# Hybrid decoder block: every engine and the load queue held to the order in which the kernel is written

## The chip, the cores and the metric

The kernel runs on one core of one Trainium2 chip. The metric is device time in microseconds (us) of one execution; several executions are timed and their median is given. One execution was profiled besides, and its trace is what the rows below come from. A core has TensorE (PE, with its weight loads PEld), VectorE (DVE), ScalarE (ACT), GpSimd (POOL) and SyncE (SP), which here issues nearly all DMAs and is called the load queue.

## The reference

One decoder block on 512 tokens of width 2048, behind 16 meta tokens, in fp32. Two branches share one input projection; their outputs are merged by sigmoid gates and projected.

```python
u = rmsnorm(h, norm_g)                      # h = [meta | x], 528 tokens
q, k, v, g_att, z_ssm, xbc, dt, m_att, m_ssm = split(u @ w_in)
# differential attention, 8 heads, ALiBi, causal; p = softmax of each of two maps
oa = rmsnorm(einsum(p[0] - lam * p[1], v), subln_g) * (1 - lam_init)
y_att = (oa * silu(g_att)) @ w_br_attn
# SSD (Mamba-2), 32 heads, chunks of 128 tokens
xbc = silu(causal_conv4(xbc) + conv_b)
xs, bm, cm = split(xbc)
dtf = softplus(dt + dt_bias)
ys = ssd_chunked(xs, dtf, -exp(a_log), bm, cm) + xs * d_skip
y_ssm = rmsnorm_groups(ys * silu(z_ssm), ssm_norm_g) @ w_br_ssm
h = h + (sigmoid(m_att) * y_att + sigmoid(m_ssm) * y_ssm) @ w_out
out = rmsnorm(h[16:], final_g)
```

## The kernel before

**Dense work.** All weights lie in one array of tiles of 128x1024, loaded by the load queue into five buffers `w` (`pump`, `release`). A product in fp32 is three matmuls: each operand is split into a high part and a remainder, and high*high, high*low and low*high are summed in PSUM. `split` (L173, L174) makes `wh` on ScalarE and `wl` on VectorE for half a tile, five buffers each; `xsplit` (L438, L439) does the same for the token operands `xv`. A job of most matrices is one level of Strassen (`strassen`): seven products P1 to P7 over quarter operands B11, B12, B21, B22 and their differences T1 to T4, with weight sums S on VectorE (L184, L187). A unit is half a product, 12 matmuls (L310); a `plain` job has units of 24 (L354).

**Order of the work.** `dense` runs a job's units through a look-ahead: two units have their weight sums written ahead (SUMS), three their weight split (LOOK), then the unit's matmuls are written. `later(fn, n)` writes a function n units on; side work (attention heads, the SSD chunks) is a list of generators, `tasks`, and one or more steps of them are written behind each unit. `flush` empties the look-ahead, `drain` the side tasks; a stage ends with them, and a stage's set-up code follows. The context is built with `TileContext(schedule_with_timeline_sim=True)`: what is written is a sequence for each engine, but a scheduler chooses in which order each engine issues its instructions.

**Stages** in the profile's time: token norms and q/k/v/gate jobs with eight attention heads beside them (up to some 600 us), the convolution jobs (to some 860), z jobs with the SSD chunks beside (to some 1340), the last gate jobs, the jobs ya (attention branch) and ys (SSM branch, to some 1620), the out jobs, and the final norm.

**Places that the change and the prediction touch.**
- `token_scale(n)`: squares of the tokens on ScalarE (L508), power -0.5 on POOL, a broadcast by TensorE (L527), a copy to `y` on ScalarE (L529); then VectorE scales the quarters `q_B..` (L541) and `xsplit` splits them.
- `attn_out`: squares of the head's output (L783), sums (L786 to L788), power on POOL (L789), scaling to `og` (L792), transposes by TensorE (L796), gating (L798). `head_tasks` puts a head's steps into `tasks`; `run_unit` posts it six units after the head's last dense unit. `qk_parts` splits q and k.
- the set-up of the SSD stage (L897 to L961): constants, `dt` loaded back (L913), transposes (L922, L924), softplus as a series on VectorE (L925 to L946), cumulative sums by TensorE (L948, L949), exponentials, transposes (L958), a copy and a store (L960, L961). It is written between the convolution's `flush` and the first z job.
- `ssd_group`/`chunk`: a chunk's decay matrices `mm` on ScalarE (L1049, eight, with six more ScalarE operations in the same step).
- `ssm_operands`: side task beside the ya jobs that loads and splits the ys jobs' operands. `out_operand`: splits the out jobs' operands from the merged tiles `mq` (m11, m12, m21, m22); the first six of eight rows of each quarter are split during the last ys job, the rest behind it.

```python
def out_operand(v, *parts):
...
        for o in parts:
            if p is not None:
                (psub if v in ("T2", "T3") else vsub)(d[:, o], p[:, o], m[:, o])
            xsplit(xo[v], d[:, o], o, pool if v == "B22" and o.start == 0 and p is None else dve)
```

## Time and profile before

| | before |
|---|---|
| time, median of 3 runs | 1818.43 us (1816.68 to 1822.35) |
| profiled execution: time, span | 1816.67 us, 1815.0 us |
| mean granted clock of TensorE | 0.973 of full speed |
| instructions | 35924 |
| TensorE / VectorE / ScalarE / POOL busy | 94% / 86% / 53% / 14% of the span |
| chain that ended last | TensorE 68%, VectorE 18%, DMA 5% |

The span is from the first to the last instruction of the profiled execution. Busy time of TensorE is modelled from its records, so busy does not mean full rate: a lower granted clock shows as the same busy time with fewer matmuls. Names in rows are the program's tiles, output before the arrow; L310 is line 310 of the kernel before.

### The profile page before, as it was taken

What the parts mean: (1) busy time and instruction counts of PE and PEld (TensorE: products, weight loads), DVE (VectorE), ACT (ScalarE), POOL (GpSimd) and SP (SyncE); (2) the same over time, 40 slices, a digit from 0 to 9 for tenths busy, and PEclk for the clock granted to TensorE, in tenths of its full rate; (3) what the DMA queues carried; (4) which work ended last, traced back from release to release, by engine and by line L of the source; (5) the groups of instructions that cost most, each with busy time, mean ns of one, the idle gap of its engine ahead of it and who ended that gap; (6) DMA issues with size and microseconds to landing.
All of it is one profiled execution on the core that took longest, in us unless ns stands there. A gap on an engine that the chain in (4) does not pass through costs nothing.

```text
span 1815.0 us, 35924 instructions
## 1 busy us (share of the span) xinstructions
PE 1707.7 (94%) x13547; PEld 1639.2 (90%) x13547; DVE 1565.0 (86%) x3004; ACT 969.2 (53%) x1961; POOL 262.1 (14%) x241
## 2 busy tenths in 40 slices
PE   5999999999999799999998999999998999989995
PEld 4999988988989799999997889989998999989995
DVE  6898878887888699999988888988978499999996
ACT  6555545554565355555576665555553254455553
POOL 0000000000000000000013431121302012235443
PEclk9999989998999899999999999999999999999998
DMA  7332212221223134333556555455466545433433
GB/s 298 134 113 82 88 64 88 70 89 65 88 76 106 66 129 129 129 118 129 154 172 177 172 156 171 158 169 167 127 231 228 186 144 171 153 114 106 139 117 105
DMA packets 136765, 244.10 MB, mean 134 GB/s; under 512 B 15088, under 2 KB 78768, under 8 KB 136080
## 3 DMA queue, kind: packets, MB, share of 16 engines
q1 hardware_dynamic: 136592, 241.81, 40.9%
q8 instruction: 107, 1.75, 0.4%
q14 instruction: 66, 0.54, 0.1%
HBM read 207.88 MB, written 33.88 MB: 133 GB/s over the span
## 4 chain that ended last, share of the span: by engine, by line
PE 68%; DVE 18%; DMA 5%; issue 4%; ACT 4%; POOL 1%; SPq 0%; DVEq 0%; ACTq 0%; POOLq 0%
PE d_ps L310 53%; PE d_ps L354 6%; DVE wl L174 5%; DMA w<-in_w_all 2%; DVE w L184 2%; DVE cv L865 2%; DMA mm<-d_acs 2%; PE s_ps L722 1%; ACT wh L173 1%; DVE S L187 1%; PE o_ps L770 1%; ACT mm L1049 1%; DVE u L187 1%; PE s_ps L719 1%; DVE S L184 1%
## 5 line engine op out<-in xcount | busy, mean ns | idle before, releaser
L310 PE MATMUL d_ps<-x,wh 128*128 128x256 f32 (+1 forms) x4160 | 772.2, 286 | 16.2 <-ACT x L438 5.9
L310 PEld LDWEIGHTS d_ps<-x,wh 128*128 128x128 f32 x4160 | 647.9, 191 | 24.7 <-ACT x L438 6.3
L173 ACT ACTIVATE wh<-w 128x512 fp32r<-128x512 f32 x706 | 438.3, 628 | 407.1 <-PE d_ps L310 263.0
L310 PE MATMUL d_ps<-x,wl 128*128 128x256 f32 (+1 forms) x2080 | 593.1, 287 | 11.1 <-DVE wl L174 10.7
L174 DVE TENSOR_TENSOR wl<-w,wh 128x512 fp32r<-128x512 f32 x706 | 506.5, 729 | 109.7 <-ACT wh L173 105.5
L310 PE MATMUL d_ps<-y,wh 128*128 128x256 f32 (+1 forms) x3120 | 585.8, 287 | 8.4 <-ACT wh L173 5.2
L310 PEld LDWEIGHTS d_ps<-y,wh 128*128 128x128 f32 x3120 | 488.3, 191 | 18.9 <-ACT wh L173 8.0
L310 PE MATMUL d_ps<-y,wl 128*128 128x256 f32 (+1 forms) x1560 | 444.4, 287 | 0.6 <-DVE wl L174 0.5
L310 PEld LDWEIGHTS d_ps<-x,wl 128*128 128x128 f32 x2080 | 393.7, 190 | 17.9 <-DVE wl L174 15.0
L310 PEld LDWEIGHTS d_ps<-y,wl 128*128 128x128 f32 x1560 | 296.1, 191 | 3.9 <-DVE wl L174 1.7
L173 ACT ACTIVATE wh<-S 128x512 fp32r<-128x512 f32 x260 | 158.7, 627 | 154.6 <-PE d_ps L310 73.5
L174 DVE TENSOR_TENSOR wl<-S,wh 128x512 fp32r<-128x512 f32 x260 | 182.3, 716 | 23.6 <-ACT wh L173 21.5
L354 PE MATMUL d_ps<-x,wh 128*128 128x256 f32 x704 | 129.3, 284 | 2.1 <-DVE cth L1170 1.1
L354 PEld LDWEIGHTS d_ps<-x,wh 128*128 128x128 f32 x704 | 109.5, 191 | 3.3 <-ACT y L438 1.3
L354 PE MATMUL d_ps<-x,wl 128*128 128x256 f32 x352 | 99.2, 286 | 5.5 <-DVE wl L174 5.4
L184 DVE TENSOR_TENSOR S<-S,w 128x512 f32<-128x512 f32 x130 | 94.6, 766 | 0.0
L184 DVE TENSOR_TENSOR w<-w 128x512 f32<-128x512 f32 x130 | 92.3, 719 | 0.0
L184 DVE TENSOR_TENSOR w<-w,S 128x512 f32<-128x512 f32 x130 | 88.3, 693 | 1.1
L187 DVE TENSOR_TENSOR S<-w 128x512 f32<-128x512 f32 x130 | 86.8, 707 | 2.4 <-DMA w<-in_w_all 2.0
L789 POOL TENSOR_TENSOR ssq<-ssq,mhalf 128x4 f32<-128x4 f32 x8 | 8.1, 1007 | 514.2 <-DVE ssq L788 514.2
L354 PEld LDWEIGHTS d_ps<-x,wl 128*128 128x128 f32 x352 | 66.4, 190 | 6.6 <-DVE wl L174 6.2
L190 POOL TENSOR_TENSOR mq<-mq,cth 128x256 f32<-128x256 f32 x32 | 36.5, 1152 | 194.5 <-DVE mq L187 191.0
(258 smaller groups left out, 1849.2 us busy)
## 6 DMA issues: line engine op xcount, KB each, us to landing
w<-in_w_all SPq DMA_DIRECT2D x291, 512.0 KB, 3.6
mm<-d_acs SPq DMA_DIRECT2D x16, 512.0 KB, 6.5
d_x<-cv SPq DMA_DIRECT2D x24, 264.0 KB, 2.0
q_B<-in_xT SPq DMA_DIRECT2D x8, 528.0 KB, 11.8
d_tha<-gth SPq DMA_DIRECT2D x16, 256.0 KB, 3.1
lx<-d_x SPq DMA_DIRECT2D x16, 256.0 KB, 4.5
d_sz<-gth SPq DMA_DIRECT2D x16, 256.0 KB, 4.3
lz<-d_sz SPq DMA_DIRECT2D x16, 256.0 KB, 3.5
```

The lines of the kernel that those rows point to most:

```text
L173: act.activation(h[:, :n], src, AF.Copy)
L174: dve.tensor_tensor(l[:, :n], src, h[:, :n].bitcast(F32), ALU.subtract)
L184: dve.tensor_tensor(dst, a, b, ALU.subtract)
L187: dve.tensor_tensor(dst, a, b, ALU.add)
L190: pool.tensor_tensor(dst, a, b, ALU.mult)
L310: pe.matmul(ps[:, :width], lhsT=a[:, ks], rhs=x[:, kk, lo:lo + width], start=(kk == 0 and i == 0), stop=(kk == kp - 1 and i == 2))
L354: pe.matmul(b[:, :width], lhsT=a[:, cs], rhs=x[:, ki, lo:lo + width], start=(first and k == 0 and i == 0), stop=(last and k == 1 and i == 2))
L719: pe.matmul(ps[:, :b - a], lhsT=qs[:, m, rows], rhs=ks[:, m, a:b], start=True, stop=False)
L722: pe.matmul(ps[:, :b - a], lhsT=qs[ms, m, rows], rhs=kl[ms, a:b], start=False, stop=True)
L770: pe.matmul(o_ps[:, i, :], lhsT=at[:, j, :], rhs=vt[:, j, :], start=(j == 0), stop=False)
L865: dve.scalar_tensor_tensor(v, raw[:, j:j + L], cw[:, ft, j:j + 1], v, ALU.mult, ALU.add)
L1049: act.activation(mm[:, h, :], mm[:, h, :], AF.Relu, scale=-1.0, bias=acs[:, c, g * HPG + h:g * HPG + h + 1])
```

## The change

`InOrder` wraps the five issuing engines: each instruction gets a dependency on the one written before it on the same engine, of a class that needs no semaphore (NoSync). The scheduler may therefore no longer move an instruction past another on its engine or on the load queue. Besides, some code is written at other places: head tasks are posted four units after a head's last dense unit and not six; `qk_parts` makes k's parts first; the z job's tanh is posted two units later for one of its four quarters; the last gate job uses its seven products in another order (ORDER_LAST); the subtractions T2 and T3 of the ys and out operands, and one remainder of B22, go from POOL to VectorE; other slots hold B21 and T3 of out; B21 and B22 of the ys operands are no longer split beside the ya jobs but at units 1 to 4 of the first ys job (`soon`, `ssm_late`).

```diff
+ORDER_LAST = ("P1", "P2", "P6", "P7", "P4", "P3", "P5")
...
+class InOrder:
+
+
+    def __init__(self, tc, engine):
+        self.tc, self.engine, self.last = tc, engine, None
+
+    def __getattr__(self, name):
+        op = getattr(self.engine, name)
+
+        def issue(*args, **kw):
+            r = op(*args, **kw)
+            if self.last is not None:
+                self.tc.add_manual_dep(r.ins, self.last, mybir.DependencyInfo(
+                    mybir.DependencyClass.NoSync, mybir.DependencyReason.DATA), reason="in order")
+            self.last = r.ins.name
+            return r
+        return issue
...
-    act, dve, pool, pe, sp = nc.scalar, nc.vector, nc.gpsimd, nc.tensor, nc.sync
+    act, dve, pool, pe, sp = (InOrder(tc, nc.scalar), InOrder(tc, nc.vector), InOrder(tc, nc.gpsimd), InOrder(tc, nc.tensor), InOrder(tc, nc.sync))
...
-            later(after, 6)
+            later(after, 4)
...
-    for v in ("B11", "B22", "B21"):
+    for v in ("B11", "B21", "B22"):
...
+        act.activation(ks[lo_, 0], kT[lo_], AF.Copy)
+        act.activation(ks[hi_, 1], kT[hi_], AF.Copy)
         act.activation(qs[lo_, 0], qT[lo_], AF.Copy, scale=scale)
         act.activation(qs[hi_, 1], qT[hi_], AF.Copy, scale=scale)
-        yield
-        dve.scalar_tensor_tensor(qs[hi_, 0], qT[lo_], scale, qs[lo_, 0].bitcast(F32), ALU.mult, ALU.subtract)
-        dve.scalar_tensor_tensor(qs[lo_, 1], qT[hi_], scale, qs[hi_, 1].bitcast(F32), ALU.mult, ALU.subtract)
-        act.activation(ks[lo_, 0], kT[lo_], AF.Copy)
-        act.activation(ks[hi_, 1], kT[hi_], AF.Copy)
...
+        yield
+        dve.scalar_tensor_tensor(qs[hi_, 0], qT[lo_], scale, qs[lo_, 0].bitcast(F32), ALU.mult, ALU.subtract)
+        dve.scalar_tensor_tensor(qs[lo_, 1], qT[hi_], scale, qs[hi_, 1].bitcast(F32), ALU.mult, ALU.subtract)
...
+            def squash():
+                t = sb.tile([P, 256], F32, tag="zt", bufs=1, name="zt")
+                act.activation(t, d, AF.Tanh, scale=0.5)
+                later(lambda: gated(t))
...
-            act.activation(t, d, AF.Tanh, scale=0.5)
-            later(gated)
+            later(squash, 2 if (f, n) == (0, 1) else 0)
...
-    dense(gate_job(name, i, d_ths), before={8 + j: (lambda v=v: att_quarter(v))
+    dense(gate_job(name, i, d_ths, ORDER_LAST), before={8 + j: (lambda v=v: att_quarter(v))
...
-                             ("T3", y12, (y22, y12)), ("T4", y11, (y21, y11)), ("B21", y21, (None, None)),
-                             ("B22", y22, (None, None))):
+                             ("T3", y12, (y22, y12)), ("T4", y11, (y21, y11))):
...
-                    (psub if v in ("T3", "T2") else vsub)(d[:, o], p[:, o], m[:, o])
+                    vsub(d[:, o], p[:, o], m[:, o])
...
+        yq.update(B21=y21, B22=y22)
+
+    def ssm_late(v, o):
+
+        if v not in xv or xv[v] is not xy.get(v):
+            xv[v] = xy[v] = tuple(xslot(xb, "x", (8, 256)) for _ in range(2))
+        xsplit(xy[v], yq[v][:, o], o)
...
-            xo[v] = tuple(xslot(yp, "y", (8, 256)) if v in ("B11", "B12", "B21", "T4") else xslot(xb, "x", (8, 256))
+            xo[v] = tuple(xslot(yp, "y", (8, 256)) if v in ("B11", "B12", "T3", "T4") else xslot(xb, "x", (8, 256))
...
-                (psub if v in ("T2", "T3") else vsub)(d[:, o], p[:, o], m[:, o])
-            xsplit(xo[v], d[:, o], o, pool if v == "B22" and o.start == 0 and p is None else dve)
+                vsub(d[:, o], p[:, o], m[:, o])
+            xsplit(xo[v], d[:, o], o)
...
+    soon = {1 + 2 * j + k: (lambda v=v, k=k: ssm_late(v, slice(4 * k, 4 * k + 4)))
+            for j, v in enumerate(("B21", "B22")) for k in range(2)}
...
-        dense(ys_job(i, mq), before=early if i == 7 else None)
+        dense(ys_job(i, mq), before=soon if i == 0 else early if i == 7 else None)
```

How this moves instructions is shown at three places. In the rows of the kernel after the change each operation has the line of the wrapper (L128).

ScalarE at the start of the program, before (`y,ss<-y` are the squares of the second pair of token tiles, `x<-q_B` operand copies, `y<-s_ps` the copy of a broadcast):

```order
7 L438 ACTIVATE x<-q_B_109 128x1056
8 L173 ACTIVATE wh<-w 128x512 x2
9 L438 ACTIVATE x<-q_B_109 128x1056
10 L438 ACTIVATE x<-q_B_111 128x1056
11 L508 ACTIVATE y,ss<-y 128x1024 x2
12 L438 ACTIVATE x<-q_B_111 128x1056
13 L508 ACTIVATE y,ss<-y 128x1024 x2
14 L173 ACTIVATE wh<-w 128x512 x2
15 L277 ACTIVATE c_287<-d_ps 128x264
16 L173 ACTIVATE wh<-w 128x512 x2
17 L529 ACTIVATE y<-s_ps 128x256
```

ScalarE at the same place, after:

```order
6 L128 ACTIVATE x<-q_B_109 128x1056 x2
7 L128 ACTIVATE wh<-w 128x512
8 L128 ACTIVATE x<-q_B_111 128x1056
9 L128 ACTIVATE wh<-w 128x512
10 L128 ACTIVATE x<-q_B_111 128x1056
11 L128 ACTIVATE wh<-w 128x512 x2
12 L128 ACTIVATE y,ss<-y 128x1024 x4
13 L128 ACTIVATE y<-s_ps 128x256
```

The squares were split in two pairs around an operand copy and stood ahead of the weight copies of rows 14 and 16 before; they now stand in one piece behind both halves of operand 111 and four weight copies. On TensorE the broadcast that needs them (`s_ps<-ident,r`) stands behind 12 dense matmuls now, where 48 stood before it.

TensorE where the SSD stage is set up, before, at the second and third of the set-up's steps there (`s_ps<-dec` are the cumulative sums, `s_ps<-ident,acs` the transposes L958):

```order
4279 L310 MATMUL d_ps<-y,wh 128x256
4280 L948 MATMUL s_ps<-dec,tri 128x160
4281 L949 MATMUL s_ps<-dec,ones 128x160
4282 L310 MATMUL d_ps<-y,wh 128x256
4283 L310 MATMUL d_ps<-y,wl 128x256
...
4301 L310 MATMUL d_ps<-y,wl 128x256
4302 L958 MATMUL s_ps<-ident,acs 32x128 x4
4303 L1026 MATMUL s_ps<-ident,lx 16x128 x4
4304 L1029 MATMUL s_ps<-ident,lb 16x128
4305 L310 MATMUL d_ps<-y,wh 128x256 x2
```

TensorE at the set-up, after, with the last convolution matmuls ahead of it and the first of the z job behind it:

```order
3887 L128 MATMUL d_ps<-x,wh 128x264 x2
3888 L128 MATMUL d_ps<-x,wl 128x264
3889 L128 MATMUL s_ps<-ident,mm 16x32
3890 L128 MATMUL s_ps<-ident,mm 128x32 x4
3891 L128 MATMUL s_ps<-dec,tri 128x160
3892 L128 MATMUL s_ps<-dec,ones 128x160
3893 L128 MATMUL s_ps<-ident,acs 32x128 x4
3894 L128 MATMUL d_ps<-x,wh 128x256 x2
3895 L128 MATMUL d_ps<-x,wl 128x256
3896 L128 MATMUL d_ps<-x,wh 128x256 x2
```

Before, dense matmuls stood on both sides of each step; some 250 rows lay between L924 and L948. Now the three steps stand in one piece between the last convolution matmul (264 columns) and the first z matmul (256 columns).

VectorE between the last ys job and the first out job, before (`mq_18617` to `mq_18620` are the merged tiles, `wl` weight remainders):

```order
2302 L439 TENSOR_TENSOR x<-mq_18620,x 128x1024
2303 L184 TENSOR_TENSOR mq_18619<-mq_18618,mq_18619 128x1024
2304 L439 TENSOR_TENSOR y<-mq_18619,y 128x512
2305 L187 TENSOR_TENSOR mq_18617<-d_ps,u_20719 128x256
2306 L187 TENSOR_TENSOR mq_18620<-d_ps,u_20841 128x256
2307 L174 TENSOR_TENSOR wl<-w,wh 128x512
2308 L439 TENSOR_TENSOR y<-mq_18618,y 128x768 x2
2309 L439 TENSOR_TENSOR y<-mq_18618,y 128x512
2310 L174 TENSOR_TENSOR wl<-w,wh 128x512
2311 L187 TENSOR_TENSOR mq_18617<-mq_18617,cv 128x256
2312 L187 TENSOR_TENSOR mq_18620<-mq_18620,cv 128x256
```

VectorE at the same operations, after (`mq_18605` to `mq_18608` are the merged tiles here, and row 2376 is the first weight remainder of out):

```order
2367 L128 TENSOR_TENSOR mq_18608<-mq_18608,cv 128x256
2368 L128 TENSOR_TENSOR y<-mq_18607,y 128x512
2369 L128 TENSOR_TENSOR y<-mq_18608,y 128x512
2370 L128 TENSOR_TENSOR x<-mq_18606,x 128x512
2371 L128 TENSOR_TENSOR x<-mq_18605,x 128x512
2372 L128 TENSOR_TENSOR mq_18607<-mq_18608,mq_18607 128x1024
2373 L128 TENSOR_TENSOR x<-mq_18607,x 128x1024
2374 L128 TENSOR_TENSOR mq_18607<-mq_18608,mq_18607 128x1024
2375 L128 TENSOR_TENSOR x<-mq_18607,x 128x1024
2376 L128 TENSOR_TENSOR wl<-w,wh 128x512
2377 L128 TENSOR_TENSOR mq_18607<-mq_18605,mq_18607 128x1024
2378 L128 TENSOR_TENSOR x<-mq_18607,x 128x1024
```

The operands' subtractions and remainders now stand in one block ahead of out's first weight remainder, where weight remainders had been mixed in among them.

## Rows read from the trace of the kernel before

**Rows 1.** The page, part 1: busy us, share of the span, instructions.
```profile
PE 1707.7 (94%) x13547; PEld 1639.2 (90%) x13547; DVE 1565.0 (86%) x3004; ACT 969.2 (53%) x1961; POOL 262.1 (14%) x241
```

**Rows 2.** Stretches: us; busy PE, PEld, DVE, ACT, POOL; PE clock; DMA share, GB/s.
```profile
100.00:590.00 490.00, 475.43 (x3533) 441.63 (x3531) 398.98 (x963) 260.17 (x574) 7.05 (x7) 0.97 0.25 83
...
590.00:620.00 30.00, 18.20 (x111) 16.71 (x110) 13.21 (x35) 9.31 (x23) 1.20 (x5) 0.72 0.12 35
...
640.00:860.00 220.00, 214.11 (x1753) 212.00 (x1751) 220.00 (x425) 117.98 (x199) 1.81 (x18) 1.00 0.37 126
...
860.00:880.00 20.00, 19.16 (x162) 18.79 (x161) 19.50 (x43) 10.28 (x23) 1.09 (x2) 1.00 0.57 168
...
860.00:1340.00 480.00, 461.68 (x3773) 438.31 (x3772) 432.12 (x802) 293.86 (x669) 111.31 (x94) 0.99 0.55 166
...
1340.00:1400.00 60.00, 52.44 (x414) 51.38 (x414) 46.58 (x58) 27.04 (x43) 10.91 (x4) 0.94 0.65 229
...
1400.00:1600.00 200.00, 200.00 (x1669) 200.00 (x1669) 165.18 (x284) 83.16 (x135) 32.38 (x28) 1.00 0.49 161
...
1600.00:1620.00 20.00, 13.20 (x91) 12.28 (x90) 20.00 (x22) 8.68 (x14) 10.81 (x5) 0.83 0.25 87
...
1640.00:1660.00 20.00, 16.52 (x123) 16.14 (x123) 19.43 (x24) 11.04 (x21) 9.84 (x5) 0.91 0.33 107
```

**Rows 3.** Timeline of ScalarE, then VectorE, at the start: start us, us.
```profile
17.10 1.08 ACT L438 ACTIVATE x<-q_B 128x1056 fp32r<-128x1056 f32 x1 [1.94 <-DVE q_B L541]
...
21.32 1.04 ACT L508 ACTIVATE y<-y 128x1024 f32<-128x1024 f32 x1
...
15.37 6.55 DVE L541 SCALAR_TENSOR_TENSOR q_B<-q_B,c_norm_g,y 128x264 f32<-128x264 f32 x16
...
21.83 1.25 DVE L439 TENSOR_TENSOR x<-q_B,x 128x1056 fp32r<-128x1056 f32 x1
...
32.67 6.56 DVE L541 SCALAR_TENSOR_TENSOR q_B<-q_B,c_norm_g,y 128x264 f32<-128x264 f32 x16 [0.43 <-ACT y L529]
```

**Rows 4.** A group of TensorE instructions (L796), and one of them in the timeline.
```profile
L796 PE MATMUL s_ps<-ident,og 128*128 128x128 f32 x32 | 6.9, 353 | 16.6 <-DVE og L792 15.9 <-ACT wh L173 0.7
...
252.87 1.09 PE L796 MATMUL s_ps<-ident,og 128*128 128x128 f32 x4 [4.13 <-DVE og L792]
```

**Rows 5.** The stretch behind that stall, columns as in rows 2.
```profile
252.00:260.00 8.00, 7.13 (x24) 5.48 (x24) 4.21 (x16) 2.04 (x7) 0.00 (x0) 0.50 0.10 33
```

**Rows 6.** Timeline of the load queue, VectorE and ScalarE, 860 to 925 us.
```profile
862.89 0.43 SPq L913 DMA_DIRECT2D mm<-d_dt  x1
...
867.82 0.17 DVE L925 TENSOR_TENSOR eac<-s_ps,c_dt_bias 16x32 f32<-16x32 f32 x1
...
873.76 1.15 DVE L932 RECIPROCAL dds<-dds 128x160 f32<-128x160 f32 x1
...
910.20 0.31 DVE L946 SCALAR_TENSOR_TENSOR dec<-dtk,c_a_log 128x160 f32<-128x160 f32 x1
...
919.01 0.59 ACT L960 ACTIVATE mm<-s_ps 32x512 f32<-32x512 f32 x1 [0.99 <-PE s_ps L958]
```

**Rows 7.** DMA issues: queue, count, KB each, median us to landing.
```profile
cth<-d_tha SPq DMA_DIRECT2D x16, 256.0 KB, 3.2
...
mm<-d_dt SPq DMA_DIRECT2D x1, 66.0 KB, 2.0
```

**Rows 8.** Groups by shape: count, busy us, mean ns, idle before and its releaser.
```profile
L174 DVE TENSOR_TENSOR wl<-w,wh 128x512 fp32r<-128x512 f32 x706 | 506.5, 729 | 109.7 <-ACT wh L173 105.5 <-PE d_ps L310 0.9
...
L1049 ACT ACTIVATE mm<-mm,acs 128x128 f32<-128x128 f32 x128 | 39.8, 389 | 38.1 <-DMA mm<-d_acs 38.1
...
L439 DVE TENSOR_TENSOR x<-yq,x 128x1024 fp32r<-128x1024 f32 x8 | 11.7, 1488 | 0.0
...
L439 DVE TENSOR_TENSOR x<-mq,x 128x1024 fp32r<-128x1024 f32 x6 | 7.8, 1303 | 0.0
```

More of the change, by code (lines that the diff above doesn't have):

```diff
@@ L214, in block_kernel, with strassen @@
     parity = [0]
-    def strassen(ji, width, lo, dst, fin, end=None, first=None):
+    def strassen(ji, width, lo, dst, fin, end=None, first=None, order=ORDER):
         mat = jobs[ji][3]
@@ L317, in unit @@
             return (lambda: sums(p, u)), (lambda: prep(p, u, src)), (lambda hl: mm(p, u, *hl))
-        for part in (ORDER,) if first is None else (ORDER_FIRST, ORDER_REST):
+        for part in (order,) if first is None else (ORDER_FIRST, ORDER_REST):
             for p in part:
@@ L564, in natural, with gate_job @@
         return [(t[:, 8 * n:8 * n + 8], 0, 8), (t[:, M + 256 * n:M + 256 * (n + 1)], 8, HL)]
-    def gate_job(name, idx, spill):
+    def gate_job(name, idx, spill, order=ORDER):
         th = {}
@@ L581, in fin @@
             later(squash, 1)
-        return strassen(job_at[name, idx], 256, 8, dst, fin)
+        return strassen(job_at[name, idx], 256, 8, dst, fin, order=order)
     def plain_gate(idx):
@@ L973, in fin, with gated @@
         def fin(f, n, d):
-            t = sb.tile([P, 256], F32, tag="zt", bufs=1, name="zt")
-            def gated():
+            def squash():
+                t = sb.tile([P, 256], F32, tag="zt", bufs=1, name="zt")
+                act.activation(t, d, AF.Tanh, scale=0.5)
+                later(lambda: gated(t))
+            def gated(t):
                 dve.scalar_tensor_tensor(d, t, 1.0, d, ALU.add, ALU.mult)
@@ L1210, in ssm_operands @@
                 if p is not None:
-                    (psub if v in ("T3", "T2") else vsub)(d[:, o], p[:, o], m[:, o])
+                    vsub(d[:, o], p[:, o], m[:, o])
                 xsplit(xy[v], d[:, o], o)
                 yield
+        yq.update(B21=y21, B22=y22)
[3 more added lines that the diff above has]
+        xsplit(xy[v], yq[v][:, o], o)
+    yq = {}
     prep_ys = ssm_operands()
```

## The prediction

> **What bounds the kernel now.** The page comes first: TensorE is busy 94% of the span, VectorE 86% [rows 1]. So at most 107 us of TensorE idling can be won by any new order, plus what a lower clock costs. Then the table of stretches, to see where these 107 us lie [rows 2]. From 1400 to 1600 us TensorE is busy all the time at full clock: 1669 matmuls in 200 us, 0.12 us each, is the rate of pure dense work. Between 640 and 860 us VectorE is busy 220 of 220 us: the convolution stage is VectorE's, and order alone gives nothing there. In attention (100 to 590 us) TensorE idles 14.6 us and the clock is 0.97, some 14.7 us more; its end (590 to 620) idles 11.8. The SSD stage (860 to 1340) idles 18.3 us. The joints between stages are short of time only late: 7.6 us at 1340 to 1400, 6.8 at 1600 to 1620, 3.5 at 1640 to 1660. Around 860, where the SSD stage is set up, hardly anything is lost (0.8).
>
> **What the change does, by its steps.** The scheduler had moved instructions of later work ahead of stalled ones. In written order, a serial chain that stands between two dense jobs is laid bare at each joint, while short chains inside a stage are covered by a fixed number of dense units.
>
> *Start.* Before, the second token scale's broadcast stood behind 48 dense matmuls and ended near 32 us; VectorE went on at 32.67 [rows 3]. Now it stands behind 12, and the four squares that it needs stand on ScalarE behind two more operand copies. Half an operand costs four products (16 take 6.55, so 1.64), a copy of 1.08 and a remainder of 1.25, and VectorE waits for the copy. From 15.4: B11's halves and the first weight remainder end near 23.6, the first half of the next operand and its weight at 28.0, the second half's products at 29.7, its copy and two weight copies at 32, the squares (four of 1.04) at 36, sums and power at 38. TensorE has 12 matmuls to do until then. The other 36 last 4.3 us if all is ready, and to 46 if the halves of B12 come between as written: +11 to +14. The operand T4, now ahead of a weight remainder, adds 0 to 8. I take +16 (11 to 22).
>
> *Head ends.* Eight times the broadcast of o (L796) waits for VectorE's og, 16.6 us in all [rows 4]; one such stall of 4.13 ended at 252.9. Behind it the clock was 0.50 from 252 to 260 [rows 5]: that costs half of 8 us, about as much as the stall. After, three dense units (4.3 us) stand between L771 and L796. The chain between them took those 4.1 us; in written order weight copies and remainders of 0.6 to 0.7 stand between its steps on ScalarE and VectorE, three on its path: 6.0 us. So 1.7 us of stall stay at each of seven heads, 12 us, with up to 2.6 us of clock: 12 to 30 against 29.3. Against that stands whatever else the scheduler had covered. I take 0 (-15 to +15).
>
> *End of attention.* 11.8 us idle and a clock of 0.72 over 30 us cost about 16; after, two gaps of 2.7 and 4.3 and some clock, 11.6. -5 (-12 to 0).
>
> *Set-up of the SSD stage.* The largest term. L922 to L958 now stand before the first matmul of the z job, as the order shows. After the last convolution matmul come evacuation, taps, tanh and gate, about 9 us; on the load queue the dt load stands behind the store of that result and three loads (0.43 to 0.45 each), and lands 2.0 later [rows 6, 7]: 12.8. Transposes: 14. Then VectorE's softplus series, 22 operations from L925 to L946, most of 0.16 to 0.33 and one of 1.15: 7.2 by itself, where before it took from 867.8 to 910.2 between other work [rows 6]. At 21 come two matmuls, a copy, a subtraction, the transposes of acs and ScalarE's copy of 0.59; then the first weight copy, 23.6. Before, the dense matmuls covered all of it but 1.6. +22, and 3 us of clock, a little less than behind 252: +25 (19 to 31). What hid it was the z job's dense work, and nothing else stands there.
>
> *SSD stage.* 18.3 us idle and 0.01 of 480 us in clock, 23 in all, could go. But ScalarE's step for a chunk is written in one piece: eight of L1049 at 0.39 [rows 8], 3.1 us, and six behind them that I put at as much, about 6, against a look-ahead of three units (4.3 us) and slack on the way: about 0.7 a chunk, 11 us. With what else stays: -8 (-20 to +14).
>
> *Gate job to ya, and ya.* Before, 7.6 idle and 0.06 of 60 us in clock: 11.2. After, 3 at the emptied look-ahead, 7 where banks are evacuated late behind blocks of subtractions that moved from POOL to VectorE, 3 of clock, and 0 to 1.9 in each of eight ya jobs where a load of cth stands behind a store (its landing alone is 3.2 [rows 7]). +6 (-4 to +16).
>
> *ya to ys.* No loss stands there before. B21 and B22 are split at units 1 to 4 of the first ys job, with nothing ahead in the look-ahead: four remainders of 1.49 [rows 8], a weight sum, copy and remainder, less the 1.4 that each unit gives TensorE, about 7, with some clock. +8 (5 to 12).
>
> *ys to out.* VectorE has, between the last ys weight and the first of out, eight evacuations (0.4 by their width), four remainders of 512 columns (0.7), two subtractions and two remainders of 1024 (1.2 to 1.3) [rows 8]: 10 to 12 us of idle TensorE, since all of out's operands are needed at once. Behind the first weight remainder stand two more pairs, another 3 to 7. The emptied look-ahead after out's first job has two pairs and four evacuations, 8.5; clock 6. 32 against the 15.5 that these stretches lose before (6.8 and 3.5 idle, 0.17 and 0.09 of 20 us). +18 (10 to 26).
>
> *Convolution, the other ys jobs, tail.* VectorE's sum there stays. +2 (0 to 10).
>
> The edits that reorder the q and k parts, the tile allocations and the last gate job's products go with these sums; alone they have no price, since the work is the same and VectorE has slack wherever TensorE is at its full rate (165 of 200 us). The subtractions moved off POOL are in the joints' sums.
>
> Sum: 16 + 0 - 5 + 25 - 8 + 6 + 8 + 18 + 2 = +62. The profiled execution's own time is 1816.67 (span 1815.0 and 1.7 around it), 1.8 below the median of the runs shown; 1816.7 + 62 = 1879. The half-widths put together as independent (6, 15, 6, 6, 17, 10, 4, 8, 5) give 29: 1850 to 1908 for this case.
>
> **Rivals.** (1) The sum as it stands: bare chains at the joints outweigh what the stages win back. Chance 0.74.
>
> (2) The other side: the fixed distances remove every head-end stall, the end of attention's and the SSD stage's, 29 + 16 + 23 = 68, and the joints (start, set-up, ya to ys, ys to out: 67) cost half because the chains overlap more than I added up. 1816.7 - 68 + 34 = 1783. For it: those losses are in the rows, and the change starts a head's tasks two units earlier. Against: the chain at a head end is longer than the three units now in front of it, and the set-up has no dense work beside it. It decides as soon as the joints cost less than the stages give back. A slight gain belongs to it too. Chance 0.09.
>
> (3) The same sign, larger: every one of the many shorter stalls (1.7 at seven heads, 0.7 at sixteen chunks, up to 1.9 in eight ya jobs) is followed by a stretch at 1.2 GHz of the length seen at 252 to 260, some 4 us lost each at the seven heads. 1879 + 30 = 1909, more if the chunks join in. For it: the row at 252 [rows 5]. Against: stalls of under 1 us leave a clock of 1.00, as at 860 to 880. Chance 0.12.
> Beside this stands a rule of the Trainium skill, "TensorE: Matmul & The Clock Gate", section "HAM oscillation — how this bites in real kernels": a kernel with a wait in each of its K tiles paid the slow clock again at every one of them. The trace agrees for the 4.1 us stall; for waits of 1.7 us no run here shows it yet, and by the rule the time would be this rival's only if such waits suffice.
>
> (4) No change: the engines' written order is already nearly what the scheduler chose. Against: L958 moved across several hundred TensorE instructions. 1817. Chance 0.03. The last 0.02 are for mishaps.
>
> A measurement of this kernel tells 0.3% from no change, 5.5 us. Faster 0.09 (rival 2), same 0.04 (rival 4 and the edge of 1), slower 0.87. To leave out no more than 2 in 10, and with the unknowns that the joints hold, the range is 1836 to 1914.
>
> **What would show it.** In the new profile: no dense matmul between the last convolution product and L958's, with TensorE idle there for about 22 us and half clock behind it (wrong if under 10); idle TensorE between about 26 and 38 us (wrong if it runs on); 15 to 20 us idle where the ys jobs end; L796's waits down to 1 to 2 us each and no 4 us ones; ScalarE's weight copies late in the SSD stage by under 1 us a chunk. The prediction falls if the set-up chain turns out covered, or if head ends and SSD together return over 60 us.

## The result: 14% slower, and where the time went

The changed kernel takes 2081.42 us (median of 4 runs, 2077.25 to 2081.98) against 1818.55 us (4 runs): a ratio of 1.1438, 95% interval 1.1414 to 1.1461. The direction was forecast, the size was not: +263 us, where the prediction had +62 and a range that ended at 1914.

The page of the kernel after, part 1, and from part 2 the granted clock in 40 slices; they answer to [rows 1]:

```profile
PE 1755.8 (84%) x13547; PEld 1683.8 (81%) x13547; DVE 1582.6 (76%) x3013; ACT 959.2 (46%) x1961; POOL 212.1 (10%) x232
...
PEclk9999999999999999979898898888998999997998
```

The work is nearly the same as before (TensorE's 13547 matmuls; VectorE is busy 18 us more, POOL 50 less); the shares fall because the span grew by 265 us. Idle TensorE went from 107 us to 324 (2080.2 less 1755.8), and its mean clock from 0.973 to 0.934. Time at the lower level, twice the missing share of the span, rose from some 98 us to some 275.

To see where, the trace is cut by work and not by time: TensorE's dense matmuls (those that write `d_ps`) are 12168 in both kernels, and the start of number 672, 3360, 3696, 5040, 5712, 8736, 9744, 10752, 11088 and 12168 marks the end of a stretch. Each number below is the us from one mark to the next. The columns behind "after" are the main experiments. Stretches hold their joints: "set-up" begins with the last convolution jobs, "SSD" ends among the gate jobs, "ya" begins with the last of these, and "ys" begins with the join from ya.

| us | before | after | edits, no wrapper | PE held | DVE held | ACT held | SP held | all but SP | DVE, heads only |
|---|---|---|---|---|---|---|---|---|---|
| start | 124.5 | 154.7 | 123.0 | 133.9 | 149.2 | 132.0 | 124.0 | 153.5 | 123.9 |
| heads | 449.6 | 452.6 | 463.5 | 450.0 | 442.4 | 468.2 | 463.5 | 452.5 | 429.5 |
| end of heads | 65.1 | 41.4 | 50.1 | 40.7 | 41.3 | 40.6 | 54.5 | 41.4 | 41.2 |
| convolution | 169.4 | 188.3 | 169.4 | 170.8 | 189.0 | 169.4 | 169.2 | 189.9 | 169.6 |
| set-up | 83.8 | 118.2 | 83.8 | 114.2 | 123.9 | 112.2 | 104.1 | 116.4 | 83.8 |
| SSD | 464.6 | 581.1 | 464.3 | 536.0 | 498.1 | 475.3 | 475.7 | 522.6 | 453.4 |
| ya | 130.5 | 175.6 | 127.4 | 128.8 | 138.3 | 125.2 | 155.4 | 136.1 | 126.6 |
| ys | 121.6 | 139.9 | 121.0 | 121.0 | 121.7 | 121.0 | 121.0 | 121.1 | 121.0 |
| ys to out | 54.6 | 75.6 | 48.0 | 48.7 | 74.4 | 61.1 | 49.1 | 73.4 | 48.5 |
| out | 130.0 | 135.1 | 131.6 | 134.0 | 129.6 | 130.0 | 132.5 | 136.3 | 131.2 |

The SSD stretch alone lost 116.5 us, ya 45. Heads and their end are best read together, since the stalls at the last head lie on either side of the mark in the two kernels: they gained 20.7. Stretches of time of the kernel after, columns as in [rows 2]: the heads, the convolution, the set-up, SSD, ya, and most of out.

```profile
160.00:560.00 400.00, 378.81 (x2940) 354.67 (x2939) 337.19 (x834) 213.46 (x493) 9.07 (x7) 1.00 0.26 81
...
640.00:840.00 200.00, 185.60 (x1443) 181.43 (x1442) 187.26 (x350) 93.43 (x162) 1.62 (x16) 0.97 0.35 113
880.00:920.00 40.00, 15.69 (x99) 14.38 (x100) 26.01 (x55) 11.14 (x24) 0.50 (x2) 0.62 0.17 54
960.00:1520.00 560.00, 461.20 (x3513) 439.34 (x3514) 404.06 (x720) 281.00 (x633) 97.88 (x92) 0.90 0.44 134
1560.00:1680.00 120.00, 88.29 (x630) 85.34 (x631) 56.98 (x83) 27.56 (x40) 0.00 (x0) 0.86 0.35 113
...
1920.00:2040.00 120.00, 120.00 (x1002) 120.00 (x1001) 113.51 (x175) 69.19 (x137) 50.03 (x47) 1.00 0.38 124
```

In the SSD stage neither TensorE (82%) nor VectorE (72%) is full: they wait in turn (in the same stage before, between 860 and 1340, TensorE was busy 96%). In the heads the clock is 1.00 though TensorE idles 21 us in the 400; before, it was 0.97 with 14.6 idle in 490 [rows 2].

TensorE's waits in the whole kernel after (us in total, times, longest), the largest:

```profile
PE n_ps L128 <- POOL y L128: 52.5, 14, 8.8
PE d_ps L128 <- DVE wl L128: 45.8, 51, 5.8
PE d_ps L128 <- ACT wh L128: 34.4, 7, 13.5
PE d_ps L128 <- DVE cth L128: 30.4, 11, 7.3
PE s_ps L128 <- POOL r L128: 24.5, 2, 13.4
PE d_ps L128 <- DVE u L128: 17.5, 10, 4.3
PE n_ps L128 <- DMA mm<-d_acs: 17.1, 2, 8.7
PE s_ps L128 <- DMA mm<-d_dt: 15.9, 1, 15.9
PE s_ps L128 <- DMA lx<-d_x: 13.9, 4, 4.1
PE s_ps L128 <- DVE og L128: 11.2, 8, 2.5
```

The largest is one the prediction never named: `n_ps`, the matmul that sums a chunk's squares for the group norm (L1101 before). Its 52.5 us, and the 17.1 that a load is named for, all lie in the SSD stage, where TensorE's waits add up to 97 us. Its chain in one chunk, from the timelines of the load queue, POOL, ScalarE and TensorE:

```profile
1258.01 1.13 SPq L128 DMA_DIRECT2D d_ths<-gth  x2
1259.19 0.61 SPq L128 DMA_DIRECT2D lz<-d_sz  x1
...
1267.40 1.26 POOL L128 TENSOR_TENSOR lz<-y,lz 128x512 f32<-128x512 f32 x1 [6.70 <-DMA lz<-d_sz]
...
1268.70 0.63 ACT L128 ACTIVATE y<-lz 128x512 f32<-128x512 f32 x1 [9.70 <-POOL lz L128]
...
1271.05 0.59 PE L128 MATMUL n_ps<-ones,y 128*128 128x1 f32 x2 [8.68 <-DMA mm<-d_acs]
```

The load of the gate tile lz is issued at 1259.19, right behind two stores (and, before them, three weight tiles from 1256.37 on), and POOL's product starts at 1267.40. How much of these 8.2 us each transfer ahead of it takes is not shown. ScalarE holds the square at the head of its queue for 9.70 us, with the weight copies behind it. TensorE holds the norm's matmul for 8.68, with the dense matmuls behind that. (The releaser printed for TensorE is a load that came last by the profile; the operand is y, which POOL had just summed at 1269.40 to 1270.99.)

### The profile page after: what moved, and what is told of

Same layout as the page of the kernel before. It is cut to its first block, busy times and chain, and to the rows that moved or that the text cites. A ratio compares the mean times of both kernels' runs of the same rounds, so it can differ in the third digit from the quotient of the medians.

```text
span 2080.2 us, 35705 instructions
## 1 busy us (share of the span) xinstructions
PE 1755.8 (84%) x13547; PEld 1683.8 (81%) x13547; DVE 1582.6 (76%) x3013; ACT 959.2 (46%) x1961; POOL 212.1 (10%) x232
## 5 line engine op out<-in xcount | busy, mean ns | idle before, releaser
L128 PE MATMUL d_ps<-x,wh 128*128 128x256 f32 (+1 forms) x4896 | 937.5, 292 | 59.5 <-DVE cth L128 30.4
L128 PEld LDWEIGHTS d_ps<-x,wh 128*128 128x128 f32 x4896 | 783.5, 196 | 78.0 <-issue 44.2
L128 PE MATMUL d_ps<-x,wl 128*128 128x256 f32 (+1 forms) x2448 | 709.1, 290 | 21.6 <-DVE wl L128 21.3
L128 PE MATMUL d_ps<-y,wh 128*128 128x256 f32 (+1 forms) x3216 | 620.0, 293 | 34.8 <-ACT wh L128 22.9
L128 DVE TENSOR_TENSOR wl<-w,wh 128x512 fp32r<-128x512 f32 x706 | 511.0, 734 | 146.4 <-ACT wh L128 144.5
L128 ACT ACTIVATE wh<-w 128x512 fp32r<-128x512 f32 x706 | 429.8, 625 | 373.3 <-DVE w L128 169.4
L128 PEld LDWEIGHTS d_ps<-y,wh 128*128 128x128 f32 x3216 | 516.5, 197 | 43.7 <-ACT wh L128 23.7
L128 PEld LDWEIGHTS d_ps<-x,wl 128*128 128x128 f32 x2448 | 478.2, 195 | 28.7 <-DVE wl L128 28.6
L128 PE MATMUL d_ps<-y,wl 128*128 128x256 f32 (+1 forms) x1608 | 468.1, 291 | 24.9 <-DVE wl L128 24.5
L128 PEld LDWEIGHTS d_ps<-y,wl 128*128 128x128 f32 x1608 | 315.6, 196 | 31.9 <-DVE wl L128 31.7
L128 ACT ACTIVATE wh<-S 128x512 fp32r<-128x512 f32 x260 | 158.8, 627 | 214.1 <-DVE S L128 165.0
L128 DVE TENSOR_TENSOR wl<-S,wh 128x512 fp32r<-128x512 f32 x260 | 182.2, 707 | 65.1 <-ACT wh L128 64.3
L128 DVE TENSOR_TENSOR S<-w 128x512 f32<-128x512 f32 x130 | 96.8, 745 | 0.0
L128 DVE TENSOR_TENSOR S<-S,w 128x512 f32<-128x512 f32 x130 | 90.0, 692 | 4.5
L128 DVE TENSOR_TENSOR w<-w 128x512 f32<-128x512 f32 x130 | 93.3, 717 | 0.0
L128 DVE TENSOR_TENSOR w<-w,S 128x512 f32<-128x512 f32 x130 | 90.3, 695 | 1.8
L128 PE MATMUL n_ps<-ones,y 128*128 128x1 f32 x32 | 8.1, 321 | 69.6 <-POOL y L128 52.5
L128 PEld LDWEIGHTS n_ps<-ones,y 128*128 128x128 f32 x32 | 6.7, 261 | 72.9 <-POOL y L128 72.9
L128 POOL TENSOR_TENSOR mq<-mq,cth 128x256 f32<-128x256 f32 x32 | 28.7, 906 | 353.2 <-DMA cv<-d_t 210.8
L128 ACT ACTIVATE sc<-sc,mn 128x144 f32<-128x144 f32 (+3 forms) x64 | 36.3, 569 | 48.8 <-DVE mn L128 48.8
L128 DVE TENSOR_TENSOR cth<-d_ps,cth 128x256 f32<-128x256 f32 x32 | 12.4, 421 | 61.1 <-DMA cth<-d_tha 41.4
L128 POOL TENSOR_TENSOR ssq<-ssq,mhalf 128x4 f32<-128x4 f32 x8 | 10.1, 1260 | 466.3 <-DVE ssq L128 413.8
```

Source lines behind the costliest of these rows:

```text
L128: r = op(*args, **kw)
```

## The experiments

All numbers are one run beside a run of the kernel before (1814.4 to 1819.5), except e9, e10 and e14, which were timed in several rounds. Differences of a few us lie within the spread of the kernel before (1816.7 to 1822.4 beside the result, 1810.4 to 1821.5 beside e13 and e14). The wrapper on the kernel before without any of the edits was not tried; the edits were tried without the wrapper.

**e1, the edits without the wrapper.**

```diff
-    act, dve, pool, pe, sp = (InOrder(tc, nc.scalar), ...
+    act, dve, pool, pe, sp = nc.scalar, nc.vector, nc.gpsimd, nc.tensor, nc.sync
```

> All edits of the change, without the wrapper: the scheduler orders the engines again. Theory 'distance' (the loss comes from holding the written order, in which the work between a producer and its consumer is too short): 1800 to 1840, the SSD stage without the 52 us that TensorE stood before the norm's matmul. Rival 'edits' (the moved splits, subtractions and head tasks cost the time): over 1900.

1804.97 us, against 1816.42, as the theory 'distance' had it: the edits cost nothing. The heads are longer (463.5), their end and ys to out shorter. In the kernel with the edits the whole loss, 276 us, comes with the held order.

**e2, load queue free; e4, e5, e6, e13, one engine held and the others free.** In each, `InOrder` wraps only the engines named, for TensorE so:

```diff
+    act, dve, pool, pe, sp = (nc.scalar, nc.vector, nc.gpsimd, InOrder(tc, nc.tensor), nc.sync)
```

> The change, but the load queue is not held to the written order; the four compute engines are. Theory 'distance': loads can move ahead only where their slot is free, and the chains over POOL, ScalarE and VectorE stay: 1960 to 2050. Rival 'load queue' (loads that stand behind waiting stores carry the loss): under 1900. Rival 'compute order alone': 2070 to 2090.

> The edits of the change, and TensorE alone held to the written order. Theory 'distance': TensorE still stands at the head of its queue for the set-up chain and the norm's matmul, but loads and the other engines can run ahead: 1860 to 1960. Rival 'TensorE alone' (its order carries nearly all): over 2020. Rival 'TensorE does not matter': under 1840.

> The edits, and VectorE alone held to the written order. With the load queue free the change lost 119 us less, and TensorE alone in order lost 91 over the edits; what neither shows is the convolution stage (+19), the step from ys to out (+25) and most of the start (+20). Theory 'VectorE blocks': these 64 us are VectorE's, 1850 to 1880. Rival 'ScalarE': 1805 to 1825 here, and the 64 us appear with ScalarE alone in order.

> The edits, and ScalarE alone held to the written order. Theory 'VectorE blocks': 1800 to 1825, since ScalarE is busy 53% and its weight copies have a look-ahead of three units. Rival 'ScalarE': 1850 to 1880, with the convolution stage near 188 us (the tanh that waits for the taps stands ahead of weight copies).

> The edits, and the load queue alone held to the written order. Freed from the whole, it gave 119 us back (SSD stage 58, ya 39, ys 19). Theory 'own cost' (loads written next to their use behind waiting stores stop whoever computes): 1890 to 1930, with these three stages as long as that over the edits alone. Rival 'only together' (the free engines find other work while a load is late): 1805 to 1840, and the 119 us arise only where compute is held as well.

Measured: 1962.75 with the load queue free, 1895.68 with TensorE held, 1933.0 with VectorE, 1859.36 with ScalarE, 1873.13 with the load queue. The table above gives the stretches. Four readings:

- Convolution and ys to out belong to VectorE (189.0 and 74.4 held alone, 169.4 and 48.0 free), as does most of the start; ScalarE held alone adds 13 us to ys to out. VectorE is the bound of the convolution stage; the first row below is that stage with VectorE held, the second with the edits alone. Once its order is fixed it idles 11 of 160 us, mostly for weight copies (9.7 us); in the whole stage (636 to 829 us) it idles 13, of the 20 us that the stage grew.

```profile
640.00:800.00 160.00, 144.63 (x1127) 140.35 (x1126) 148.67 (x280) 74.66 (x129) 1.31 (x13) 0.98 0.33 109
```

```profile
645.00:800.00 155.00, 150.45 (x1227) 148.77 (x1226) 155.00 (x301) 80.77 (x135) 1.40 (x14) 1.00 0.36 126
```

- The set-up costs 20 to 40 us whichever single engine is held (104.1 to 123.9 against 83.8), and 34 with all five. This fits a chain that crosses every engine and is laid bare by any one of them.
- SSD is worst with TensorE held (+72 over the edits), then VectorE (+34); ScalarE and the load queue cost 11 each. With everything held it is +117, and freeing the load queue takes half of that away.
- The load queue alone falls between the theories: it costs 68 us, 28 of them in ya and 20 in the set-up, but only 11 in SSD and none in ys, where its release gave 58 and 19. So in SSD and ys its order costs most of that only where the waiting engines are held too.

The runs with the load queue free and with TensorE held came out within the theory 'distance', the first at its lower edge. My expectations for VectorE (1850 to 1880) and ScalarE (1800 to 1825) were both too low: I had given the set-up and SSD to TensorE alone. ScalarE's time fell into its rival's range, but not for the rival's reason, since the convolution stage stayed at 169.4.

**e3, the gate tile's load earlier.** `gz` and its load move from the chunk's fifth step to its first.

```diff
             xT, bT, cT = now["x"][:, :, :n], now["bc"][:, 0, :n], now["bc"][:, 1, :n]
+            if c > 0:
+                gz = sb.tile([P, 4, P], F32, tag="lz", bufs=2, name="lz")
+                sp.dma_start(gz, d_sz[fs_, :, (c - 1) * P:c * P].rearrange("f p t -> p f t"))
...
```

> The change, with a chunk's load of the gate tile lz written at the chunk's first step and not four steps later; nothing else moves. Theory 'distance': TensorE's wait for POOL before the norm's matmul falls from 52 us to under 15, and with the half clock behind these stalls the time falls by 45 to 90, to 1990 to 2035. Rival 'load queue' in the sense of late weight tiles, and rival 'ScalarE burst' (the step with eight decay operations delays the weight copies): no change, 2070 to 2090.

2054.08: the wait fell from 52.5 to 18.8 us (under 15 was expected), the time only by 27 and not by 45 or more; that it moved at all is against both rivals. In SSD (581.1 to 550.6) the wait for lx stayed (13.9 before the edit) and one for the decay matrices mm grew from 0.6. TensorE's longest waits from 940 to 1500 us:

```profile
PE n_ps L128 <- POOL y L128: 18.8, 11, 2.3
PE s_ps L128 <- DMA lx<-d_x: 14.5, 4, 3.9
PE s_ps L128 <- DVE mm L128: 11.1, 7, 1.8
```

**e8, more steps in the norm's tail.** Empty steps, one dense unit each: one ahead of the square, two ahead of the sum's matmul, one ahead of the broadcast.

```diff
             pmul(gz, y.rearrange("p (f t) -> p f t", f=4), gz)
             yield
             yield
+            yield
...
             padd(y[:, :P], y[:, :P], y[:, P:256])
             yield
+            yield
+            yield
...
```

> The change, with four empty steps more in each chunk's tail: the squares stand one unit later behind the gating, the norm's matmul two units later behind the sums, the broadcast one later behind the power. Theory 'distance': TensorE waits for POOL before the norm's matmul 20 us and not 52, SSD stage 581 down by 30 to 60, time 2020 to 2050. Rival 'late transfer' (the lz load, 8 us from issue to use, sets it whatever stands between): under 15 us gained.

2052.02, SSD 551.3: 30 us as with the early load, with the load where it was, so the late transfer alone does not set the time; the gain falls just short of what the theory had (2020 to 2050). The wait for the norm is gone altogether, but TensorE now stands for the decay matrices. Its longest waits from 940 to 1500 us:

```profile
PE s_ps L128 <- DVE mm L128: 27.5, 11, 4.0
PE s_ps L128 <- DMA lx<-d_x: 19.5, 4, 5.5
PE d_ps L128 <- DVE gth L128: 15.1, 5, 4.0
```

**e7, the ya jobs' loads earlier.**

```diff
-        def evac(f, n, b):
-            if n == 0:
+        def fetch():
+            for f in range(2):
                 t[f] = gp.tile([P, S], F32, tag=("cth", "cv")[idx % 2], bufs=2, name="cth")
                 sp.dma_start(t[f], d_tha[2 * idx + f])
+
+        def evac(f, n, b):
...
+        units, fetch = ya_job(i)
+        dense(units, before={2: fetch})
```

> The change, with each ya job's two loads of cth written at the job's third unit and not at the evacuation that uses them. Theory 'distance': VectorE's evacuations no longer wait for the landing, TensorE's 30 us wait for them goes and the ya stage falls from 175.6 to 130 to 145; time 2040 to 2055. Rival 'the stage is bound by the yq splits on VectorE': under 10 us gained, above 2070.

2040.96, ya 140.3 instead of 175.6, as the theory had it. This is the clean one: a load of cth stood on the load queue behind the store of the tile before it, and VectorE's evacuation behind the load. In the kernel after (load queue, then VectorE):

```profile
1599.29 0.33 SPq L128 DMA_DIRECT2D d_t<-cth  x1
1599.66 0.43 SPq L128 DMA_DIRECT2D cth<-d_tha  x1
...
1603.15 0.76 DVE L128 TENSOR_TENSOR cth<-d_ps,cth 128x256 f32<-128x256 f32 x2 [3.89 <-DMA cth<-d_tha]
```

**e11, the set-up as a side task; e12, all distances enlarged.** The set-up's code (L906 to L961) becomes a generator of 13 steps in `tasks`, beside the first z jobs, with a `yield` wherever the next engine takes over. e12 adds e3, e7, e8 and the second token pair's squares three units earlier.

```diff
+    def set_up():
...
+        pe.matmul(ps[:, 160:320], lhsT=ones.to_broadcast([P, P]), rhs=da, start=True, stop=True)
+        yield
+        dve.tensor_copy(acs, ps[:, :160])
...
+    tasks.append(set_up())
```

> The change, with the set-up of the SSD stage written as a side task of 13 steps beside the first two z jobs. Prediction's step (the bare chain costs 22 us and some clock): the set-up stretch falls from 118 to 84 to 92, time 2045 to 2058. Rival 'VectorE's backlog from the convolution keeps TensorE waiting there anyway': 105 or more, above 2068.

> The change, with all five distances enlarged together: set-up as a side task, lz at the chunk's first step, four empty steps in the norm's tail, cth at the job's third unit, and the second token pair's squares three units earlier. If the losses are separate they add up (34, 27, 29, 40 and some 5 to 10): 1935 to 1960. Rival 'one engine's backlog behind all' (a stall that goes is replaced by the next): above 1990. In either case the order in the start, the convolution stage and ahead of out, which VectorE alone showed to cost 70, stays.

e11: 2061.96, 19 less; the set-up stretch takes 105.6, so 12.6 of its 34 us came back. The stretch is the rival's (105 or more), the time lies between the two. What stays, by the timeline there: TensorE waits 9.33 us for the first weight copy of the z job, which ScalarE has behind a tanh that waits for VectorE's convolution taps, the backlog that the rival named; and 4.28 for the series, which is now spread over dense units but still first in TensorE's queue. TensorE, then ScalarE's tanh:

```profile
887.09 0.80 PE L128 MATMUL d_ps<-x,wh 128*128 128x256 f32 x2 [9.33 <-ACT wh L128]
...
908.28 0.87 PE L128 MATMUL s_ps<-dec,tri 128*128 128x160 f32 x2 [4.28 <-DVE dec L128]
...
885.88 0.64 ACT L128 ACTIVATE cth<-cv 128x528 f32<-128x528 f32 x1 [3.12 <-DVE cv L128]
```

e12: 1989.21, 92 us back where the separate runs make 117 (27, 29, 40 and 19) and the start next to nothing (154.7 to 152.2). It lies between the two theories, next to the rival's 1990: set-up and ya added up, in SSD (536.7) 30 and 30 made 44. There TensorE now waits for mm (19.6 us), lx (19.1), weight remainders (15.4) and gth (15.4).

**e9, e10, e14, the order held in the heads only.** `InOrder` gets a switch (not shown below) that is on from the first head to the drain behind the last: e9 for VectorE alone, e10 for all five, e14 for VectorE on the kernel before with only two edits (`later(after, 4)` and k's parts first).

```diff
+    InOrder.on = True
     for hd in range(NH):
...
     flush()
     drain()
+    InOrder.on = False
     atx.close()
```

> The edits, and VectorE alone held to the written order from the first attention head to the end of the attention stage; all else is the scheduler's. With VectorE in order throughout, heads and end took 483.7 us, with the scheduler 513.6. Theory 'the written order pays where only dense units stand between the steps': that gain comes alone, 1772 to 1782, faster than both kernels. Rival 'the stage only hands its time on' (what the heads gain is lost in the stage behind them): 1800 to 1810.

> As the run with VectorE in the attention stage, but all five engines are held to the written order there. By the stage table of the change (452.6 and 41.4 there against 463.5 and 50.1 with the edits alone): 1782 to 1790, a little slower than VectorE alone since TensorE then also stands for o's chain. Rival 'hands on': 1800 to 1810.

> The kernel before with only two of the edits (head tasks posted four units on, k's parts ahead of q's) and VectorE in order in the attention stage. Theory 'the gain is the attention stage's order': heads and end near 471 us as in the run with all edits, 1760 to 1775. Rival 'the other edits carry it': over 1795.

e9: 1756.31 us (5 runs), 0.9682 of before (0.9669 to 0.9695). e10: 1767.05, 0.9735 (0.9721 to 0.975). e14: 1764.08, 0.9712 (0.9679 to 0.9745). All three beat both kernels, e9 and e10 by more than I expected. e9, the stretch of the heads:

```profile
130.00:575.00 445.00, 445.00 (x3378) 411.74 (x3377) 386.38 (x953) 243.53 (x564) 10.28 (x12) 1.00 0.27 87
```

TensorE is busy for 445 of 445 us at full clock; no wait of it is left there, where the kernel before had 16.6 us at L796 [rows 4] and half clock behind [rows 5]. With all five held (e10) TensorE still stands 8.7 us for og, since it may not run dense matmuls past it. e14 takes 429.5 and 41.2 for heads and end, the same as e9, so that gain is VectorE's order there with those two edits; which of the two edits it needs was not separated. It is 44.0 of the 65.2 us by which the span of e9 is shorter than before. Some 11 more lie in the SSD stretch (453.4 against 464.6), and 9 in e14, where the order is not held; why is open.

## Why the prediction was right in direction and wrong in size

By its steps, forecast and measured (stretches of the table, after less before):

| step | forecast | measured |
|---|---|---|
| start | +16 | +30.2 |
| heads | 0 | +3.0 |
| end of heads | -5 | -23.7 |
| set-up | +25 | +34.4 |
| SSD stage | -8 | +116.5 |
| gate job to ya, and ya | +6 | +45.1 |
| ya to ys, and ys | +8 | +18.3 |
| ys to out | +18 | +21.0 |
| convolution and out | +2 | +24.0 |

The table's sum is 269; behind the last dense matmul 3.5 us are saved. The joints that the prediction priced as bare chains (start, set-up, the step to ys, ys to out) lost 104 us where it had 67. The larger part, 181 us, was lost inside SSD, ya and the convolution, which it had as a gain or nearly even. So the mechanism that it forecast gave the direction, and at most the smaller part of the loss.

The step that failed is "SSD stage": "23 in all, could go", less a ScalarE burst of 0.7 a chunk. It walked one engine and left out what the chunk's steps wait for: a load on the held load queue, POOL's products, and the norm's matmul in front of the dense work. e3 and e8, which lengthen that chain's distance at two different places, give 30 us each, and both together in e12 44 of the 117. A burst on ScalarE was not the cause: in the kernel after no wait of TensorE from 940 to 1500 us is for a weight copy, and ScalarE held alone costs 11 us (as much as the prediction put on the burst; that these 11 are the burst is not shown). Where the other 72 us lie is open; the waits left in e12 are for other chains (mm, lx, gth), and what each is worth was not tried. With the load queue free and compute held 58 remain.

"Gate job to ya, and ya" named the right mechanism (a load of cth behind a store) and mis-sized it: "0 to 1.9 in each", where VectorE stood 3.1 to 7.5 us before most of these evacuations, 35 us in all by e7; 10 of the 45 stay.

"ya to ys" was wrong as a mechanism. With all four compute engines held and the load queue free, B21 and B22 are split at the same place and ys takes 121.1 us, as before. So the 18.3 us come with the load queue's order, beside held compute engines. In the kernel after TensorE has short waits for weight remainders all through ys, and VectorE stands for the loads of the merge; the largest of VectorE's waits from 1720 to 1840 us (in total, times, longest):

```profile
DVE mq L128 <- DMA cv<-d_t: 12.1, 3, 4.6
```

"Convolution ... VectorE's sum there stays. +2" is wrong as reasoning: that the bound engine's sum stays says nothing of what it waits for in a fixed order (+20 with VectorE alone held). "ys to out" was right: VectorE held alone gives its loss.

"Start" was right up to 38 us: the broadcast was issued at 37.92 in the kernel after, forecast some 38. Behind it the price was too small: a stall of 9.99 us was not in it, nor the clock (0.89 from 24 to 56 us). TensorE's rows there:

```profile
22.81 0.81 PE L128 MATMUL d_ps<-x,wh 128*128 128x264 f32 x2 [7.67 <-ACT wh L128]
...
37.92 1.22 PE L128 MATMUL s_ps<-ident,r 128*128 128x128 f32 x4 [11.17 <-POOL r L128]
50.55 0.80 PE L128 MATMUL d_ps<-x,wh 128*128 128x256 f32 x2 [4.30 <-DVE u L128]
...
112.39 0.81 PE L128 MATMUL d_ps<-y,wh 128*128 128x264 f32 x2 [9.99 <-ACT gth L128]
```

"Set-up" was right in mechanism and in size within its range but for 3 us, though e11 shows that dense work beside the chain does not hide all of it: there 9.33 us are the end of the convolution. The idle time in the kernel after, in rows that answer to [rows 6]:

```profile
894.42 0.64 PE L128 MATMUL s_ps<-ident,mm 32*16 32x32 f32 x5 [15.89 <-DMA mm<-d_dt]
903.33 0.87 PE L128 MATMUL s_ps<-dec,tri 128*128 128x160 f32 x2 [8.28 <-DVE dec L128]
905.15 1.04 PE L128 MATMUL s_ps<-ident,acs 128*32 128x128 f32 x4 [0.42 <-DVE acs L128]
907.39 0.80 PE L128 MATMUL d_ps<-x,wh 128*128 128x256 f32 x2 [1.20 <-ACT wh L128]
```

15.89 + 8.28 + 0.42 + 1.20 is 25.8, and the clock is 0.62 from 880 to 920 us.

"Head ends" held in its stalls: L796 waits 11.2 us in eight, 1.2 to 1.3 in each of seven, where 12 in seven were forecast, and the last head's two gaps are 2.47 and 5.78, where 2.7 and 4.3 were. But "with up to 2.6 us of clock" did not come at the seven: the clock stays at 1.00 from 160 to 560 us. The 20.7 us that heads and end gained are clock: TensorE idles 30.6 us there (154.7 to 648.7) and idled 26.4 before (124.5 to 639.3), while the clock rose from 0.95 to 0.99. The last head's gaps and the clock behind them, then the clock behind two stalls of 1.7 us in the convolution stage, which ended at 683.28 and 848.08:

```profile
592.34 0.63 PE L128 MATMUL s_ps<-ident,og 128*128 128x128 f32 x4 [2.47 <-DVE og L128]
599.00 0.59 PE L128 MATMUL d_ps<-x,wl 128*128 128x264 f32 x1 [5.78 <-DVE wl L128]
...
595.00:605.00 10.00, 6.00 (x27) 6.00 (x28) 6.97 (x13) 2.17 (x4) 0.20 (x4) 0.50 0.08 22
...
683.00:693.00 10.00, 9.10 (x50) 8.91 (x51) 9.76 (x20) 4.55 (x8) 0.01 (x1) 0.66 0.26 79
848.00:858.00 10.00, 9.29 (x75) 9.11 (x75) 9.76 (x20) 4.25 (x8) 0.00 (x0) 1.00 0.29 82
```

So rival 3's mechanism, half clock behind every short stall, did not come where it was priced, at seven heads with stalls of 1.2 to 1.3 us. It is not refuted for its own 1.7: behind one of these two stalls the clock fell, behind the other it did not. In the SSD stage, with stalls up to 8.8 us, the clock fell to 0.90 on the mean; there the rule of the Trainium skill that the prediction set beside it ("TensorE: Matmul & The Clock Gate", section "HAM oscillation — how this bites in real kernels") agrees with the trace, a wait in each chunk and the lower clock again and again. The clock is the smaller part there too: of the 117 us, 85 are idle TensorE (from 893 to 1357 us before, 955 to 1536 after) and 32 longer busy time.

Rival 2, on the other side, was half right as a mechanism: heads and their end do gain (20.7 us in the change, 44.0 with VectorE held there alone), but that could not outweigh the joints and the other stages.

Some of the prediction's own figures do not close, by under 5 us each: with the clock charged as at its other joints, "End of attention" lost 20 before and not 16; the parts of "Gate job to ya" make +9 at their middle and not +6; 32 less 15.5 is 16.5 and not 18; the series has 21 operations on VectorE and not 22. None of this bears on an error of 200 us.

## What to carry to other kernels

In this kernel a written order paid most where dense work stands between the steps of a chain, and cost most where the whole chain from a producer to its consumer, transfers and their queue included, was longer than the work between. Walk such a chain over every engine and the load queue, from the load's issue to the last consumer, before holding an order; the engine that looks slack in the sum is no guide (POOL was busy 10%, and its result ended TensorE's largest wait). Hold the order stage by stage and engine by engine: here VectorE in one stage gained 3%, all five in that stage gained nearly as much, and all five in all stages lost 14%.

## What the runs showed of the hardware

Seven stalls of TensorE of 1.2 to 1.3 us at the ends of heads left the granted clock at 1.00 (160 to 560 us). Behind a stall of 1.7 us in the convolution stage it was 0.66 over 10 us, behind another of the same length 1.00, so the length of one stall did not decide it here. Two stalls of 2.47 and 5.78 us close together had 10 us at 0.50 with them; before, one of 4.13 was followed by 8 us at 0.50. Of the 265 us that the span grew, 217 are idle TensorE; the other 48 are the longer busy time of the same 13547 matmuls, with more of them at the lower clock.
